# Four small moves in a hybrid encoder block: activation sums, their splits, branch inputs, and an inverse root

## The chip, the cores and the metric

The kernel runs on one core of one Trainium2 chip, as a single launch. The metric is the device time of one execution in microseconds (us). The four names that come up all the time are the engines of the core: PE (TensorE, matmul), DVE (VectorE), ACT (ScalarE) and SP (SyncE, whose queue issues nearly all DMAs of this kernel).

## The reference, cut to what matters

One encoder block on a sequence of 1024 tokens of width 1024, in float32. A normalised input is projected by one wide matrix, the pieces feed a gated linear attention (GLA, branch A) and a windowed softmax attention (SWA, branch B), two sigmoid gates merge the branches, and a SwiGLU follows.

```python
h = rms_norm(x, norm_mix_g)
(g_q, g_k, g_v, g_r, g_lr_f, g_lr_b, s_q, s_k, s_v, gate_a, gate_b) = split(h @ w_in)
y_gla = gla(g_q, g_k, g_v, log gates from g_lr_f and g_lr_b)   # chunks of 64, both directions
y_gla = (rms_norm(y_gla, out_g) * silu(g_r)) @ w_o_gla
y_swa = windowed_softmax_attention(rope(rms_norm(s_q)), rope(rms_norm(s_k)), s_v, sinks) @ w_o_swa
x = x + (sigmoid(gate_a) * y_gla + sigmoid(gate_b) * y_swa) @ w_out
x = x + (silu(h2 @ w_gate) * (h2 @ w_up)) @ w_ffn_out           # h2 = rms_norm(x, norm_ffn_g)
```

## The kernel before

**Matmuls.** Float32 operands are split into a high part `h` (a copy by ACT, rounded to the matmul's type) and a low part `l` (the rest, a subtraction by DVE); a product is three matmuls, high by high, high by low, low by high. A weight tile of 128x512 is loaded (`wr`), split into `wh` and `wl` (`wunit`, L66 to L71) and used. The normalised input lies in 16 pairs of tiles `xh{k}{s}`, `xl{k}{s}` (k is one of 8 blocks of channels, s one of two halves of the tokens).

**Order of the work.** The order of PE's instructions is the order of the program (a manual schedule for PE alone). The orders of DVE, ACT and SP are set by the tile scheduler, which places each instruction by its own model; so an edit can move instructions far from where they are written. Each engine then works through its list in order, and so does SP's queue: a DMA that waits for its data or for a free buffer holds back the DMAs listed after it.

**Dense work as filling.** The wide projections stand in a list `dense` of generators. `fill(n)` takes n matmuls from it; `slot(stages, n)` spreads n such matmuls between the parts of an attention slot. The list ends with `first_halves`, the first half of the gate projections.

**GLA.** 24 dense matmuls run first (`fill(24)`), then the slots. In the first 8 slots `x_sums(t)` loads blocks of x, normalises them (`x_norm`) and forms five sets of sums and differences of blocks (T1, T2, 22, T3, T4) that a Strassen-like scheme needs later; each result goes to memory.

**SWA.** 22 slots; in the last four (t of 18 and more) the stages of the attention drain out, with 15 dense matmuls in each.

**Second halves of the gates.** The five sets, four tiles of 128x512 each, are loaded from memory and split (`xpart`): ACT makes `xh`, DVE `xl`. Before, the sets T1, T2 and 22 are loaded right behind the attention, with `fill(4)` after each tile; then the rest of the dense work; then `second_first(0)`, which loads and combines three weight tiles (`r11`, `r21`, `r22`) and multiplies with T1; then the sets T3 and T4; then eight rounds of `second_rest(f)`. Each round multiplies with T2, 22, T3 and T4 in turn, by weights that DVE combines from the raw ones (`comb`, L808) and `wsplit` splits (ACT L794, DVE L795). `second_rest(f)` calls `second_first(f + 1)` near its end.

**Branch inputs.** After each round, `prep_a(0, f)` loads one tile of GLA's output and one of its gate projection r into two of the four `stage` buffers, takes a sigmoid on ACT (L895), multiplies twice on DVE (L896, L897) and splits the product into `oah`, `oal`. `branch_a`, which comes right after the eight rounds, multiplies by all eight such tiles.

**The inverse root** `rsqrt` (L95 to L102) takes a logarithm and an exponential on ACT and then one Newton step on DVE. It runs twice on 128x512 at the start, and on small tiles in every GLA and SWA unit.

Of the kernel before, what the change touches and what calls it, by code (L numbers as in the profile page):

```python
# [32 lines left out]
def body(tc, i, out):  # L33
    nc = tc.nc
    with ExitStack() as root:
# [8 lines left out]
        def nm(s):  # L44
            uid[0] += 1
            return f"{s}_{uid[0]}"
# [4 lines left out]
        def chtile(shape, dt=F32):  # L51
            return psc.tile(list(shape), dt, tag="ch", name=nm("ch"))
# [41 lines left out]
        def rsqrt(dst, v, scale, epsv, eps_t, pool, shape, tag):  # L94
            l = pool.tile(list(shape), F32, tag=tag + "l", name=nm("rl"))  # L95
            nc.scalar.activation(l, v, AF.Ln, bias=eps_t[:, 0:1], scale=scale)
            nc.scalar.activation(l, l, AF.Exp, scale=-0.5)
            t = pool.tile(list(shape), F32, tag=tag + "t", name=nm("rt"))
            nc.vector.tensor_scalar(t, v, scale, epsv, op0=ALU.mult, op1=ALU.add)
            nc.vector.tensor_tensor(t, t, l, op=ALU.mult)  # L100
            nc.vector.scalar_tensor_tensor(t, t, -0.5, l, op0=ALU.mult, op1=ALU.mult)
            nc.vector.scalar_tensor_tensor(dst, t, 1.5, l, op0=ALU.add, op1=ALU.mult)  # L102


        xstack = ExitStack()
        stg = root.enter_context(tc.tile_pool(name="stg", bufs=4))
        pad = root.enter_context(tc.tile_pool(name="pad", bufs=1, side="right"))
        pad.tile([P, PAD // 4], F32, tag="pad", name="pad")
        xp = xstack.enter_context(tc.tile_pool(name="xp", bufs=1, side="right"))
        xh = [[xp.tile([P, HT], FR, tag=f"xh{k}{s}", name=f"xh{k}{s}") for s in range(2)] for k in range(KT)]  # L110
        xl = [[xp.tile([P, HT], FR, tag=f"xl{k}{s}", name=f"xl{k}{s}") for s in range(2)] for k in range(KT)]

        scr = {}
# [6 lines left out]
        glas = ExitStack()  # L120
# [133 lines left out]
        dense = []  # L254

        def fill(n):

            while n > 0 and dense:
                try:
                    next(dense[0])  # L260
                    n -= 1
                except StopIteration:
                    dense.pop(0)

        def share(plan, t):
            return next(n for end, n in plan if t < end)
# [48 lines left out]
        xr = {}  # L315
# [237 lines left out]
                  proj_t("v1", 1), proj_f("q3", 6), proj_f("k3", 7), proj_t("skv", 2), proj_t("sq0", 3),  # L553
                  proj_t("sq1", 4)] + [proj_f(f"r{m}", 8 + m) for m in range(8)] + [first_halves()]

        xn = glas.enter_context(tc.tile_pool(name="xn", bufs=4))
        part = {}

        def x_norm(k, s):
            t = xn.tile([P, HT], F32, tag="xn", name=nm("xn"))  # L560
            nc.sync.dma_start(out=t, in_=i["xT"][k, s])
            nc.vector.scalar_tensor_tensor(t, t, g1[:, k:k + 1], rstd[:, s * HT:(s + 1) * HT],
                                           op0=ALU.mult, op1=ALU.mult)
            return t
# [5 lines left out]
        def x_sums(j):  # L570
            k, late = divmod(j, 2)
            if not late:
                a, b = part[k] = x_norm(k, 0), x_norm(k, 1)
                x_diff("xT1", k, b, b, a)
                return
            a, b = part.pop(k)
            c = x_norm(k + 4, 1)
            put(("x22", k), c)
            x_diff("xT2", k, b, c, b)
            x_diff("xT3", k, a, b, a)  # L580
            c = x_norm(k + 4, 0)
            x_diff("xT4", k, c, c, b)
# [10 lines left out]
                    at[t, j + (j == 4 and c % 2)] = (f, hd, c)  # L593
                last = max(last, t)
        with tc.manual_schedule(engines={mybir.EngineType.PE}):
            fill(24)
            for t in range(last + 1):
                if t < 8:
                    x_sums(t)
                slot([(lambda v=at[t, j]: v[0](*v[1:])) if (t, j) in at else None for j in (0, 5, 4, 3, 2, 1)], share(GF, t))  # L600
        glas.close()


# [150 lines left out]
        def a_out(g, n):  # L754
# [7 lines left out]
            for h in range(4):  # L762
                nc.sync.dma_start(out=scr["b", 4 * g + h, n // 4][:, (n % 4) * P:(n % 4 + 1) * P],
                                  in_=ob[:, h])

        todo = [[] for _ in range(2 * KT + 6)]
        for n in range(2 * KT):
            g, t = divmod(n, KT)
# [9 lines left out]
        with tc.manual_schedule(engines={mybir.EngineType.PE}):  # L778
            for t, v in enumerate(todo):
                v.sort(key=lambda e: order.index(e[0]))  # L780
                slot([lambda e=e: e[0](*e[1:]) for e in v], share(SF, t))
        swas.close()

        wq = root.enter_context(tc.tile_pool(name="wq", bufs=1))
# [4 lines left out]
        tp = tps.enter_context(tc.tile_pool(name="tp", bufs=1))  # L789
# [21 lines left out]
        def product(o, w, x, nk, start, stop):  # L811
            h, l = w
            for kk in range(nk):
# [1 line left out]
                nc.tensor.matmul(o, h[:, c], x[kk][0], start=start and kk == 0, stop=False, skip_group_check=True)  # L815
                nc.tensor.matmul(o, h[:, c], x[kk][1], start=False, stop=False, skip_group_check=True)  # L816
                nc.tensor.matmul(o, l[:, c], x[kk][0], start=False, stop=kk == nk - 1, skip_group_check=True)  # L817

        XT = {q: [] for q in ("T1", "T2", "22", "T3", "T4")}
        raws = []  # L820

        def xsplit(pool, th, tl, src):
            h = pool.tile([P, HT], FR, tag=th, name=nm(th))
            l = pool.tile([P, HT], FR, tag=tl, name=nm(tl))
            nc.scalar.activation(h, src, AF.Copy)
            nc.vector.tensor_tensor(l, src, h.bitcast(F32), op=ALU.subtract)
            return h, l

        homes = {"T1": (xp, "xh{}1", "xl{}1", 0), "22": (xp, "xh{}1", "xl{}1", 4), "T2": (tp, "t2h{}", "t2l{}", 0),
                 "T3": (xp, "xh{}0", "xl{}0", 0), "T4": (xp, "xh{}0", "xl{}0", 4)}  # L830

        def xpart(q, k):
            r = tp.tile([P, HT], F32, tag="xr", name=nm("xr"), bufs=8)
            nc.sync.dma_start(out=r, in_=scr[f"x{q}", k])
            pool, th, tl, d = homes[q]
            XT[q].append(xsplit(pool, th.format(k + d), tl.format(k + d), r))

        def ntile():
            return tp.tile([P, HT], F32, tag="nt", name=nm("nt"), bufs=6)
# [8 lines left out]
        def second_first(f):  # L848
# [5 lines left out]
            g.Z = chtile((P, HT))  # L854
            product(g.Z, wsplit(g.s1, 512), XT["T1"], 4, True, False)

        def second_rest(f):
            nme, m, a, b = PAIRS[f]
            g = pend.pop(f)
            p1 = ntile()  # L860
            nc.sync.dma_start(out=p1, in_=scr[f"{nme}{m}", "p1"])
            r12 = rawload(i["w_f"][a, 1], False)
            p5 = ntile()
            nc.vector.tensor_tensor(p5, g.Z, p1, op=ALU.add)
            X = mmtile()
# [12 lines left out]
            product(X, wsplit(g.r22, 512), XT["T4"], 4, False, True)  # L878
            result((f"{nme}{m + 4}", 0), X, p1)
# [9 lines left out]
        def prep_a(s, k):  # L889
            o = stage()  # L890
            nc.sync.dma_start(out=o, in_=scr["o", k, s])
            r = stage()
            nc.sync.dma_start(out=r, in_=scr[f"r{k}", s])
            sg = btile("sg", bufs=1)
            nc.scalar.activation(sg, r, AF.Sigmoid)  # L895
            nc.vector.tensor_tensor(r, r, sg, op=ALU.mult)  # L896
            nc.vector.scalar_tensor_tensor(o, o, og[:, k % 2:k % 2 + 1], r, op0=ALU.mult, op1=ALU.mult)  # L897
            oa[s].append(split_in(bo, o, "oa", k))

        with tc.manual_schedule(engines={mybir.EngineType.PE}):  # L900
            for q in ("T1", "T2", "22"):
                for k in range(4):
                    xpart(q, k)
                    fill(4)
            fill(1 << 30)
            second_first(0)
            for q in ("T3", "T4"):
                for k in range(4):
                    xpart(q, k)
            for f in range(len(PAIRS)):  # L910
                second_rest(f)
                prep_a(0, f)
        tps.close()
        xstack.close()

# [443 lines left out]
```

## Time and profile before

| What | Number |
|---|---|
| median of 3 runs | 1684.49 us (1682.74 to 1684.93) |
| profiled execution, its own time | 1679.58 us |
| its span in the trace | 1677.3 us, so 2.28 us lie around it |
| PE busy, share of the span | 1655.2 us, 99% |
| matmuls | 7788 |
| DVE, ACT busy | 1237.9 us (74%), 857.1 us (51%) |
| mean granted PE clock | 0.996 |

A busy PE says little by itself here, since a matmul's end is modelled and a matmul at half the clock counts as busy too. What is to be read is the number of matmuls in a stretch: where PE is never held up, 20 us hold some 90 of them.

### The profile page before, as it was taken

The numbers are of one execution on the slowest core, as the hardware profiler recorded it, in microseconds if no ns is written. First come the engines' busy times: TensorE is split into PE (matmuls) and PEld (weight loads), VectorE is DVE, ScalarE is ACT, GpSimd is POOL, SyncE is SP. The second block draws the span as 40 slices with busy tenths as digits, with TensorE's granted clock in tenths as the row PEclk, the third lists the DMA queues.
The fourth block names the chain that finished last, engine by engine and source line by source line (L and its number), as shares of the span: only waits on it lengthen the run. The fifth ranks groups of instructions, "written<-read, shape, count | busy, mean of one in ns | idle before, by whom it ended". The sixth has DMA issues, their size and how long they took to land.

```text
span 1677.3 us, 23798 instructions
## 1 busy us (share of the span) xinstructions
PE 1655.2 (99%) x7788; PEld 1372.9 (82%) x7788; DVE 1237.9 (74%) x2570; ACT 857.1 (51%) x1809; POOL 0.2 (0%) x4
## 2 busy tenths in 40 slices
PE   9999999999999998999999999999999999999999
PEld 6788888887888876887888888788888888888887
DVE  8786777853997767876673568887778877789755
ACT  7454677865687674334553556533333333344443
POOL 0000000000000000000000000000000000000000
PEclk9999999999999999999999999999999999999999
DMA  8875656668533238656764545344224543595433
GB/s 286 297 259 186 200 185 227 226 196 284 185 108 107 82 113 285 227 193 214 217 213 143 190 134 180 113 136 134 91 92 144 164 157 131 177 323 192 143 102 119
DMA packets 183547, 300.13 MB, mean 179 GB/s; under 512 B 20894, under 2 KB 46238, under 8 KB 183424
## 3 DMA queue, kind: packets, MB, share of 16 engines
q1 hardware_dynamic: 183424, 298.62, 54.4%
q8 instruction: 61, 1.00, 0.3%
q14 instruction: 62, 0.51, 0.1%
HBM read 203.12 MB, written 95.42 MB: 178 GB/s over the span
## 4 chain that ended last, share of the span: by engine, by line
PE 91%; DVE 3%; DMA 3%; ACT 2%; issue 1%; SPq 0%; ACTq 0%; DVEq 0%
PE mm L75 35%; PE ch L75 8%; PE mm L815 7%; PE mm L816 7%; PE mm L817 7%; PE mm L1177 7%; PE ch L1177 5%; PE ch L815 3%; PE ch L817 3%; PE ch L816 3%; PE mm L244 2%; PE ch L747 1%; DMA xr<-xT 1%; PE ch L546 0%; PE ch L697 0%
## 5 line engine op out<-in xcount | busy, mean ns | idle before, releaser
L69 ACT ACTIVATE wh<-wr 128x512 fp32r<-128x512 f32 x198 | 123.8, 628 | 115.1 <-PE mm L75 84.5
L71 DVE TENSOR_TENSOR wl<-wr,wh 128x512 fp32r<-128x512 f32 x198 | 135.7, 686 | 32.0 <-ACT wh L69 29.1
L794 ACT ACTIVATE wh<-ws 128x512 fp32r<-128x512 f32 x120 | 75.5, 631 | 148.7 <-PE mm L816 84.6
L75 PE MATMUL mm<-wl,xh 128*128 128x512 f32 x320 | 127.0, 397 | 1.2 <-DMA wl<-wl 1.2
L75 PE MATMUL mm<-wh,xh 128*128 128x512 f32 x320 | 127.7, 399 | 0.4 <-DVE st L136 0.4
L75 PE MATMUL mm<-wh,xl 128*128 128x512 f32 x320 | 127.9, 400 | 0.0
L75 PE MATMUL mm<-xh,wh 128*128 128x512 f32 x256 | 102.5, 401 | 0.3 <-ACT wh L69 0.3
L75 PE MATMUL mm<-xl,wh 128*128 128x512 f32 x256 | 102.0, 398 | 0.3 <-DVE xl L323 0.3
L794 ACT ACTIVATE wh<-wr 128x512 fp32r<-128x512 f32 x60 | 37.9, 632 | 105.4 <-issue 49.6
L795 DVE TENSOR_TENSOR wl<-ws,wh 128x512 fp32r<-128x512 f32 x120 | 82.1, 685 | 12.8 <-ACT wh L794 12.8
L75 PE MATMUL mm<-xh,wl 128*128 128x512 f32 x256 | 88.6, 399 | 0.0
L794 ACT ACTIVATE wh<-a 128x512 fp32r<-128x512 f32 x66 | 41.7, 632 | 90.6 <-PE mm L1177 42.4
L795 DVE TENSOR_TENSOR wl<-a,wh 128x512 fp32r<-128x512 f32 x66 | 45.5, 690 | 39.2 <-ACT wh L794 38.1
L75 PEld LDWEIGHTS mm<-wl,xh 128*128 128x128 f32 x320 | 60.5, 189 | 12.6 <-DMA wl<-wl 1.6
L75 PEld LDWEIGHTS mm<-wh,xh 128*128 128x128 f32 x320 | 60.7, 190 | 10.5 <-DVE st L136 0.8
L1177 PE MATMUL mm<-hh,wh 128*128 128x512 f32 x176 | 68.6, 390 | 0.5 <-DVE c L1115 0.5
L75 PEld LDWEIGHTS mm<-wh,xl 128*128 128x128 f32 x320 | 60.7, 190 | 10.2
L1177 PE MATMUL mm<-hl,wh 128*128 128x512 f32 x176 | 68.5, 389 | 0.0
L1177 PE MATMUL mm<-hh,wl 128*128 128x512 f32 x176 | 68.5, 389 | 0.0
L1150 DVE TENSOR_TENSOR hl<-hr,hh 128x512 fp32r<-128x512 f32 x77 | 52.7, 686 | 6.8 <-ACT hh L1149 6.7
L75 PEld LDWEIGHTS mm<-xl,wh 128*128 128x128 f32 x256 | 48.2, 188 | 7.6 <-DVE xl L323 0.6
L75 PEld LDWEIGHTS mm<-xh,wh 128*128 128x128 f32 x256 | 48.2, 188 | 7.4 <-ACT wh L69 0.5
(546 smaller groups left out, 4875.0 us busy)
## 6 DMA issues: line engine op xcount, KB each, us to landing
wr<-in_w_fi_dram SPq DMA_DIRECT2D x102, 256.0 KB, 2.8
wr<-in_w_f_dram SPq DMA_DIRECT2D x80, 256.0 KB, 3.4
wh<-wh SPq DMA_DIRECT2D x80, 256.0 KB, 2.9
wl<-wl SPq DMA_DIRECT2D x80, 256.0 KB, 3.0
B<-c SPq DMA_DIRECT2D x44, 256.0 KB, 2.1
T<-st SPq DMA_DIRECT2D x44, 256.0 KB, 2.6
a<-in_w_fo_dram SPq DMA_DIRECT2D x44, 256.0 KB, 5.3
hr<-T SPq DMA_DIRECT2D x44, 256.0 KB, 2.7
```

The costliest lines, as they stand in the source:

```text
L69: nc.scalar.activation(h, raw, AF.Copy)
L71: nc.vector.tensor_tensor(l, raw, h.bitcast(F32), op=ALU.subtract)
L75: nc.tensor.matmul(o, a, b, start=start, stop=stop)
L244: nc.tensor.matmul(Y[q], w[:, c], x, start=f0, stop=f1, skip_group_check=True)
L747: nc.tensor.transpose(pt[:, h], a.p[:, h, (kb - a.b0) * P:(kb - a.b0 + 1) * P], ident)
L794: nc.scalar.activation(h, src, AF.Copy)
L795: nc.vector.tensor_tensor(l, src, h.bitcast(F32), op=ALU.subtract)
L815: nc.tensor.matmul(o, h[:, c], x[kk][0], start=start and kk == 0, stop=False, skip_group_check=True)
L816: nc.tensor.matmul(o, h[:, c], x[kk][1], start=False, stop=False, skip_group_check=True)
L817: nc.tensor.matmul(o, l[:, c], x[kk][0], start=False, stop=kk == nk - 1, skip_group_check=True)
L1150: nc.vector.tensor_tensor(l, r, h.bitcast(F32), op=ALU.subtract)
L1177: nc.tensor.matmul(ys[m], a[:, c], b, start=f0, stop=f1, skip_group_check=True)
```

## The change

1. `rsqrt` makes its Newton step with three DVE instructions in place of four.
2. The pool `xn` (four buffers of 128x512) lives through the whole kernel rather than through GLA alone, and the eight `xr` buffers for the five sets are gone: the sets are now loaded into the four `xn` buffers.
3. GLA starts with `fill(36)` in place of `fill(24)`. `x_sums` is called one slot later, behind the slot rather than ahead of it.
4. T1 and 22 (two of the five sets) are loaded and split in the four drain slots of the softmax attention. Behind the attention only T2 is loaded, with `fill(8)` after each tile.
5. `prep_a(0, f)` is called ahead of `second_rest(f)` rather than behind it, and `prep_a(0, 7)` together with `prep_a(0, 6)`, so the last round runs behind the last branch input.

```diff
-            nc.vector.tensor_scalar(t, v, scale, epsv, op0=ALU.mult, op1=ALU.add)
-            nc.vector.tensor_tensor(t, t, l, op=ALU.mult)
-            nc.vector.scalar_tensor_tensor(t, t, -0.5, l, op0=ALU.mult, op1=ALU.mult)
+            nc.vector.scalar_tensor_tensor(t, l, -0.5 * scale, l, op0=ALU.mult, op1=ALU.mult)
+            nc.vector.scalar_tensor_tensor(t, v, epsv / scale, t, op0=ALU.add, op1=ALU.mult)
             nc.vector.scalar_tensor_tensor(dst, t, 1.5, l, op0=ALU.add, op1=ALU.mult)
...
+        xn = root.enter_context(tc.tile_pool(name="xn", bufs=4))
...
-        xn = glas.enter_context(tc.tile_pool(name="xn", bufs=4))
...
-            fill(24)
+            fill(36)
             for t in range(last + 1):
-                if t < 8:
-                    x_sums(t)
                 slot([...], share(GF, t))
+                if 1 <= t <= 8:
+                    x_sums(t - 1)
...
         def xpart(q, k):
-            r = tp.tile([P, HT], F32, tag="xr", name=nm("xr"), bufs=8)
+            r = xn.tile([P, HT], F32, tag="xn", name=nm("xn"))
             nc.sync.dma_start(out=r, in_=scr[f"x{q}", k])
...
                 slot([lambda e=e: e[0](*e[1:]) for e in v], share(SF, t))
+                if t >= 2 * KT + 2:
+                    assert len(dense) == 1
+                    for q in ("T1", "22"):
+                        xpart(q, t - 2 * KT - 2)
...
-            for q in ("T1", "T2", "22"):
-                for k in range(4):
-                    xpart(q, k)
-                    fill(4)
+            homes["T2"] = tp, "t2h{}", "t2l{}", 0
+            for k in range(4):
+                xpart("T2", k)
+                fill(8)
             fill(1 << 30)
             second_first(0)
             for q in ("T3", "T4"):
                 for k in range(4):
                     xpart(q, k)
             for f in range(len(PAIRS)):
+                if f < 7:
+                    prep_a(0, f)
+                if f == 6:
+                    prep_a(0, 7)
                 second_rest(f)
-                prep_a(0, f)
```

Where the scheduler puts things now is seen at three places.

The first is SP's queue between the attention and the first round. The rows are DMAs, out<-in. Rows of the loads that fetch the sets read `xr<-` before and `xn<-` after (`x_..` is the set 22, `xT_..` the other sets); `wr`, `wr_2...` are weight tiles; `gb_...` are stores of dense results. Before, with the last weight load of `second_first(0)` (`wr_8871`) and the first of `second_rest(0)` (`wr_2162`, r12):

```order
L250 DMA gb_p_8835<-st_8833 128x512
L803 DMA wr_8871<-in_w_f_dram 128x512
L834 DMA xr_8894<-xT_0_721 128x512
L834 DMA xr_8900<-xT_1_933 128x512
L250 DMA gb_0_8851<-st_8849 128x512
L834 DMA xr_8906<-xT_2_1219 128x512
L834 DMA xr_8912<-xT_3_1504 128x512
L250 DMA gb_0_8867<-st_8865 128x512
L834 DMA xr_8918<-xT_0_727 128x512
```

After, with the same weight loads as `wr_8827` and `wr_2167`:

```order
L249 DMA gb_p_8614<-st_8612 128x512
L822 DMA wr_8827<-in_w_f_dram 128x512
L249 DMA gb_p_8648<-st_8646 128x512
L861 DMA nt_8910<-ga_p_8056 128x512
L777 DMA xn_8850<-xT_0_920 128x512
L777 DMA xn_8856<-xT_1_1202 128x512
L249 DMA gb_0_8670<-st_8668 128x512
L777 DMA xn_8862<-xT_2_1493 128x512
L777 DMA xn_8868<-xT_3_1757 128x512
L822 DMA wr_2167_8912<-in_w_f_dram 128x512
```

Behind `gb_p_8634`, the store that corresponds to `gb_p_8614`, the queue before had twelve loads of T1, T2 and 22 and five more stores ahead of `wr_8871`; now the weight load is the very next DMA. The load of r12, which stood behind all eight loads of T3 and T4, stands behind the four of T3. The loads of T1 and 22 are up in the attention and in GLA, and their splits on ACT and DVE lie between earlier units of the attention, before the four drain slots.

The second is ACT between the last rounds and branch A. `sg` is the sigmoid, `oah` the high part of a branch input, `wh<-ws` and `wh<-wr_2...` belong to the rounds, the other `wh<-wr` to branch A. Before:

```order
L794 ACTIVATE wh_9909<-wr_2365_9785 128x512
L69 ACTIVATE wh_9981<-wr_9979 128x512
L69 ACTIVATE wh_9999<-wr_9997 128x512
L895 ACTIVATE sg_9830<-st_9828 128x512
L69 ACTIVATE wh_10022<-wr_10020 128x512
L825 ACTIVATE oah_2376_9834<-st_9826 128x512
L69 ACTIVATE wh_10040<-wr_10038 128x512
L69 ACTIVATE wh_10063<-wr_10061 128x512
L69 ACTIVATE wh_10081<-wr_10079 128x512
L895 ACTIVATE sg_9933<-st_9931 128x512
L825 ACTIVATE oah_2400_9937<-st_9929 128x512
```

After:

```order
L895 ACTIVATE sg_9670<-st_9668 128x512
L813 ACTIVATE wh_9835<-ws_9833 128x512
L768 ACTIVATE oah_2350_9674<-st_9666 128x512
L895 ACTIVATE sg_9682<-st_9680 128x512
L813 ACTIVATE wh_9857<-ws_9855 128x512
L768 ACTIVATE oah_2355_9686<-st_9678 128x512
L813 ACTIVATE wh_9877<-wr_2375_9765 128x512
L69 ACTIVATE wh_9937<-wr_9935 128x512
L69 ACTIVATE wh_9955<-wr_9953 128x512
```

The last two branch inputs came behind weight splits of branch A; now they come ahead of the last round's final three weight splits.

The third is SP between GLA and the softmax attention, where constants of the attention (`cosb` to `sink`), the first keys (`kvr`) and the re-read weights of the projection `sq1` (`wl_..<-wl_2`) stand behind stores of GLA's output. Before, from the first constant on:

```order
L62 DMA cosb<-in_c_cos_dram 128x512
L62 DMA sinb<-in_c_sin_dram 128x512
L62 DMA band<-in_c_band_dram 128x384
L62 DMA qg<-in_qg_dram 128x128
L62 DMA kg<-in_kg_dram 128x128
L62 DMA sink<-in_sink_dram 128x8
L663 DMA kvr_5663<-skv_3683 128x512
L220 DMA sq_0_5704<-st_5705 128x512
L220 DMA sq_1_5714<-st_5715 128x512
L220 DMA sq_2_5724<-st_5725 128x512
L220 DMA sq_3_5734<-st_5735 128x512
L168 DMA wl_5744<-wl_2_5377 128x512
```

After:

```order
L219 DMA sq_0_5595<-st_5596 128x512
L219 DMA sq_1_5693<-st_5694 128x512
L219 DMA sq_2_5703<-st_5704 128x512
L62 DMA cosb<-in_c_cos_dram 128x512
L62 DMA sinb<-in_c_sin_dram 128x512
L62 DMA band<-in_c_band_dram 128x384
L62 DMA qg<-in_qg_dram 128x128
L62 DMA kg<-in_kg_dram 128x128
L62 DMA sink<-in_sink_dram 128x8
L661 DMA kvr_5667<-skv_3606 128x512
L219 DMA sq_3_5713<-st_5714 128x512
L167 DMA wl_5723<-wl_2_5314 128x512
```

Three stores of `sq1` now stand ahead of the constants, and `wl_2` still behind all of them. On PE the dense work is 12 matmuls further on when GLA ends. At the start of GLA, the matmul of the gates (`ch<-lrS,upS`) stands behind 36 dense matmuls rather than 24.

More of the change, by code (lines that the diff above doesn't have):

```diff
@@ L764, in a_out, with xsplit, xpart @@
                                   in_=ob[:, h])
+        XT = {q: [] for q in ("T1", "T2", "22", "T3", "T4")}
+        def xsplit(pool, th, tl, src):
+            h = pool.tile([P, HT], FR, tag=th, name=nm(th))
+            l = pool.tile([P, HT], FR, tag=tl, name=nm(tl))
+            nc.scalar.activation(h, src, AF.Copy)
+            nc.vector.tensor_tensor(l, src, h.bitcast(F32), op=ALU.subtract)
+            return h, l
+        homes = {"T1": (xp, "xh{}1", "xl{}1", 0), "22": (xp, "xh{}1", "xl{}1", 4),
+                 "T3": (xp, "xh{}0", "xl{}0", 0), "T4": (xp, "xh{}0", "xl{}0", 4)}
+        def xpart(q, k):
+            r = xn.tile([P, HT], F32, tag="xn", name=nm("xn"))
+            nc.sync.dma_start(out=r, in_=scr[f"x{q}", k])
+            pool, th, tl, d = homes[q]
+            XT[q].append(xsplit(pool, th.format(k + d), tl.format(k + d), r))
         todo = [[] for _ in range(2 * KT + 6)]
@@ L817, in product @@
                 nc.tensor.matmul(o, l[:, c], x[kk][0], start=False, stop=kk == nk - 1, skip_group_check=True)
[L819 to L832, printed above, removed]
-            r = tp.tile([P, HT], F32, tag="xr", name=nm("xr"), bufs=8)
-            nc.sync.dma_start(out=r, in_=scr[f"x{q}", k])
-            pool, th, tl, d = homes[q]
-            XT[q].append(xsplit(pool, th.format(k + d), tl.format(k + d), r))
         def ntile():
```

## The prediction

> **What bounds the kernel now.** First the page's busy row, then the waits of PE, then PE's matmuls in stretches of 20 us.
>
> ```profile
> PE 1655.2 (99%) x7788; PEld 1372.9 (82%) x7788; DVE 1237.9 (74%) x2570; ACT 857.1 (51%) x1809; POOL 0.2 (0%) x4
> PE ch L815 <- ACT wh L794: 4.6, 2, 2.6
> PE mm L75 <- ACT oah L825: 3.2, 1, 3.2
> PE ch L75 <- DVE lrS L313: 1.9, 1, 1.9
> PE mm L75 <- DMA wl<-wl: 1.2, 1, 1.2
> PE ch L75 <- ACT ph L750: 1.2, 1, 1.2
> 40.00:60.00 20.00, 17.76 (x73) 14.01 (x73) 16.67 (x34) 9.00 (x16) 0.00 (x0) 0.91 0.76 271
> 640.00:660.00 20.00, 17.55 (x77) 13.90 (x76) 15.27 (x25) 10.44 (x18) 0.00 (x0) 1.00 0.92 307
> 660.00:680.00 20.00, 17.42 (x60) 13.41 (x61) 18.18 (x30) 11.31 (x19) 0.00 (x0) 0.83 0.94 312
> 700.00:720.00 20.00, 20.00 (x90) 16.56 (x89) 17.14 (x28) 6.96 (x11) 0.00 (x0) 1.00 0.51 170
> 780.00:800.00 20.00, 16.66 (x66) 13.43 (x67) 13.70 (x21) 10.71 (x18) 0.00 (x0) 0.91 0.85 269
> ```
>
> PE bounds the kernel, and the change removes no matmul, so all that can be won is time in which PE stands still or runs slowly. In a wait row the numbers are the sum, how often, and the longest, in us. The five rows are the longest waits of PE. In a stretch the number behind `x` after PE's busy time is its matmuls, and the third number from the end is the granted clock. Undisturbed, 20 us hold 90 matmuls, 0.222 us each. From 640 to 680 there are 77 + 60, 43 too few, worth 43 x 0.222 = 9.6 us; from 780 to 800 there are 24 too few, 5.3 us; from 40 to 60 there are 17 too few, 3.8 us. That is 18.7 us, while the waits in those places add up to 4.6 + 3.2 + 1.9 = 9.7. Most of the rest is the clock behind the waits, seen in shorter stretches:
>
> ```profile
> 49.65:53.06 3.41, 3.41 (x10) 2.64 (x9) 3.38 (x6) 0.73 (x2) 0.00 (x0) 0.50 0.87 308
> 660.64:664.05 3.41, 3.41 (x10) 2.63 (x9) 2.61 (x5) 1.52 (x4) 0.00 (x0) 0.50 1.00 275
> 670.88:674.29 3.41, 3.41 (x9) 2.67 (x9) 3.41 (x7) 3.38 (x5) 0.00 (x0) 0.50 0.90 272
> 783.52:786.93 3.41, 3.19 (x8) 2.48 (x8) 2.99 (x6) 2.71 (x5) 0.00 (x0) 0.50 0.74 208
> 412.00:415.41 3.41, 2.21 (x10) 1.50 (x10) 2.84 (x12) 0.50 (x2) 0.00 (x0) 1.00 0.96 318
> 700.00:703.41 3.41, 3.41 (x16) 2.82 (x15) 3.37 (x6) 1.71 (x3) 0.00 (x0) 1.00 0.32 119
> ```
>
> Behind each of four waits the clock is halved for 3.41 us, and 8 to 10 matmuls go through where 16 would: on the mean 27 / 4 x 0.222 = 1.5 us lost. The wait at 412 to 414 left the clock at 1.00.
>
> **The splits and the first round (640 to 680).** SP's queue and the work behind the two waits of 4.6 us:
>
> ```profile
> 638.47 0.32 SPq L250 DMA_DIRECT2D gb_p<-st  x1
> 638.96 1.30 SPq L834 DMA_DIRECT2D xr<-xT  x3
> 652.43 0.42 SPq L803 DMA_DIRECT2D wr<-in_w_f_dram  x1
> 662.07 1.85 SPq L803 DMA_DIRECT2D wr<-in_w_f_dram  x4
> 657.26 0.69 DVE L808 TENSOR_TENSOR ws<-wr,wr 128x512 f32<-128x512 f32 x1
> 658.04 0.63 ACT L794 ACTIVATE wh<-ws 128x512 fp32r<-128x512 f32 x1 [2.04 <-DVE ws L808]
> 664.54 2.29 DVE L826 TENSOR_TENSOR xl<-xr,xh 128x512 fp32r<-128x512 f32 x3 [0.16 <-ACT xh L825]
> 667.94 0.68 DVE L808 TENSOR_TENSOR ws<-wr,ws 128x512 f32<-128x512 f32 x1
> 668.72 1.23 ACT L794 ACTIVATE wh<-ws 128x512 fp32r<-128x512 f32 x2 [2.62 <-DVE ws L808]
> ```
>
> PE waits for `wh`, ACT for `ws`, DVE for a weight tile that SP issues at 652.43, behind twelve loads of sets that began at 638.96. In the new order it is the DMA right behind the store of 638.47: it can start some 13 us sooner, and the first wait goes. The second wait is for r12, in the group issued at 662.07 behind all loads of T3 and T4, and for the three `xl` of 664.54 that DVE takes ahead of `ws`. In the new order r12 stands behind four loads, and the eight splits of T1 and 22 are off this stretch altogether: 8 x 0.63 us of ACT (the row of 658.04) and 8 x 0.69 us of DVE. I take both waits and both clock losses as gone: 43 matmuls, 9.6 us, less 0.3 for small ones: 9.3 us. What is late next is T3 and T4, which now share four buffers, so a load waits for a split. T4's first product comes three products (3 x 12 matmuls, 8 us) behind the round's first, and a load with its split takes some 4 to 6 us (652.43 to 658.04), so they fit with little to spare. The first `prep_a`, two loads, a sigmoid and three DVE operations, now falls into this stretch too, where DMA is 0.94 busy.
>
> The moved splits need cover inside the attention:
>
> ```profile
> 580.00:600.00 20.00, 20.00 (x104) 16.73 (x103) 14.60 (x44) 11.69 (x30) 0.00 (x0) 1.00 0.28 84
> 591.26 0.56 DVE L715 CUSTOM_DVE_ANT_0 p<-ch,band 128x384 f32<-128x384 f32 x1 [2.04 <-PE ch L75]
> 596.28 0.60 ACT L700 ACTIVATE sqh<-ch 128x512 fp32r<-128x512 f32 x1 [2.35 <-PE ch L697]
> 440.00:460.00 20.00, 20.00 (x109) 17.25 (x108) 19.78 (x84) 14.06 (x43) 0.00 (x0) 1.00 0.32 94
> ```
>
> From 580 to 600 DVE is free for 5.4 us and ACT for 8.3, in idle pieces of about 2 us, and PE never stops; 5.5 us of DVE over three or so such slots costs nothing. Were they to fall where DVE is full (440 to 460, 19.78 of 20), each would delay the attention by 0.69 us. The final waits for `ph` in the drain (1.2 us) stay: the order of ACT around them is as it was.
>
> **The branch inputs (780 to 800).**
>
> ```profile
> 777.28 2.90 DMA st<-r
> 780.26 0.63 ACT L895 ACTIVATE sg<-st 128x512 f32<-128x512 f32 x1 [1.86 <-DMA st<-r]
> 782.44 0.63 ACT L825 ACTIVATE oah<-st 128x512 fp32r<-128x512 f32 x1 [1.55 <-DVE st L897]
> ```
>
> The last `prep_a` is one chain: load of r, sigmoid, two products, split; PE waits 3.2 us for it. In the new order the last two such chains start a full round earlier (48 matmuls, 48 x 0.222 = 10.7 us), where 3.2 us sooner would do. Both run side by side with all four `stage` buffers, which holds the stores of the round, not PE. All of it goes: 24 matmuls, 5.3 us, less 0.1.
>
> **The start (40 to 60).**
>
> ```profile
> 31.28 0.69 DVE L99 TENSOR_SCALAR rt<-ch 128x512 f32<-128x512 f32 x1
> 47.14 1.21 DVE L313 TENSOR_TENSOR lrS<-lrf,lrS 32x1024 fp32r<-32x1024 f32 x1
> 48.50 0.47 PE L75 MATMUL ch<-lrS,upS 98*128 98x256 f32 x2 [1.89 <-DVE lrS L313]
> ```
>
> Behind the 24 dense matmuls PE waits 1.89 us for `lrS`, ready at 47.14 + 1.21 = 48.35. Twelve more matmuls fill 12 x 0.222 = 2.7 us, which leaves 0.8 us to spare. DVE also has two operations of 0.69 us less to do ahead of `lrS`, which only adds to that. Wait and clock go: 17 matmuls, 3.8 us, of which I take 3.5, since short matmuls are among the missing. The small `rsqrt` calls save one short DVE instruction each; where DVE is not what PE waits for that is nothing, and I count 0.
>
> **What gets worse: the entry to the attention.**
>
> ```profile
> 404.07 0.33 SPq L62 DMA_DIRECT2D cosb<-in_c_cos_dram  x1
> 407.55 2.39 SPq L220 DMA_DIRECT2D sq<-st  x4
> 409.99 4.30 DMA wl<-wl
> 414.33 0.50 PE L75 MATMUL mm<-wl,xh 128*128 128x512 f32 x1 [1.20 <-DMA wl<-wl]
> ```
>
> PE waits here for a low weight tile, issued at 409.99 behind constants whose first (404.07) follows GLA's last output. With the dense work 12 matmuls ahead, PE wants that tile 2.7 us sooner, at 414.33 - 1.20 - 2.7 = 410.4. The tile's load comes sooner by less: three of the four stores that took 2.39 us move ahead of the constants, so I put its issue at 408 to 409 (404.07, seven DMAs to 407.55, then one store) and its landing, 4.30 us on, at 412.3 to 413.3. PE then waits 1.9 to 2.9 us in place of 1.2. From 1.9 us on the clock fell in this trace (the wait for `lrS`), at 1.2 it did not, so another 1.5 goes with it. The bounds are 0.7 without the clock and 3.2 with it; I take 2.4: a wait of 2.1, since the fourth store's data come sooner as well, and the clock.
>
> **The sum.** 9.3 + 5.2 + 3.5 - 2.4 = 15.6 us less. On the profiled execution that is 1679.58 - 15.6 = 1664.0. The median of the runs stands 4.9 above that execution, so on its basis it is 1684.49 - 15.6 = 1668.9 us. A measurement tells about 0.2%, 3.4 us, from no change.
>
> **The rivals.** (a) *One wait in the splits stays.* For it: T3 and T4 go through four buffers beside the first `prep_a`, with DMA at 0.94. Against it: the margin above. One such wait with its clock is half of 9.6 (4.8), so 1668.9 + 4.8 = 1673.7. (b) *The drain or the start gives nothing.* A split put ahead of the last `ph` would add its 0.6 to 0.7 us to a wait of 1.2, and past 2 us add the clock, 1.5; or the start's wait moves to the next gates. That costs 2.2 to 3.5: 1671 to 1672. (c) *The longer wait at the entry leaves the clock whole.* It then costs 0.9 us (2.1 in place of 1.2), and the time is 1684.49 - 18.0 + 0.9 = 1667.4. For it: the wait of 1.2 did so; against it: the one of 1.9 did not. [...] (d) *The weight load does not move in time*: if SP is held at the store of 638.47 or by a buffer, the 9.3 us stay and the time is 1678. (e) *Slower.* The splits sit in ACT's and DVE's order ahead of the parts that PE waits for, and a set's load that SP cannot issue until a split frees a buffer holds the weight loads behind it. If each of the eight splits stopped PE for a load of 3 us and halved the clock (1.5), that is 8 x 4.5 = 36 us, and the time 1684.5 + 36 - 15.6 = 1705. It decides once each split costs over 2 us. The idle pieces of 2 us in both engines speak against it.
>
> **How the numbers follow.** The forecast has 0.45, (c) 0.13, (a) 0.19, (b) 0.12, (d) 0.05, (e) 0.06. Cases (a) to (c) and the forecast are faster, 0.89; (d), 6.5 us below, is faster as well in most runs, so 0.92 faster; 0.03 within 0.2%, from a mild (e); 0.05 slower. The range reaches from 1663, which is (c) less 4 us (the runs before spread by 2.2, and the profiled execution stands 4.9 below their median), to (d), 1678.
>
> **What would show it.** PE's waits for `wh` at the first round, for `oah` and for `lrS` gone, with 88 or more matmuls in each of the matching stretches; no half clock but one, near the entry to the attention; the weight load issued right behind that store; attention slots with 104 to 109 matmuls per 20 us. A half clock left between T2 and T4 would be (a); new PE waits for `sqh` or `ph` between 500 and 630 would be (e).

## The result, and the profile after

| | before | after |
|---|---|---|
| median of 4 runs | 1684.71 us (1682.74 to 1684.95) | 1669.47 us (1667.89 to 1671.38) |
| profiled execution, span | 1679.58, 1677.3 us | 1667.89, 1666.1 us |

The ratio is 0.9912, with a 95% interval of 0.99 to 0.9924: 12.8 to 16.8 us less, where 15.6 was forecast and 1668.9 us predicted. The two profiled executions lie 11.7 us apart (11.2 by their spans): that of before was shorter than all four of its runs, 5 us under their median, that of after 1.6 under.

First the busy row and PE's longest waits after the change, then the stretches that were shown of before.

```profile
PE 1650.8 (99%) x7788; PEld 1370.0 (82%) x7788; DVE 1230.9 (74%) x2525; ACT 857.0 (51%) x1809; POOL 0.2 (0%) x4
PE mm L75 <- DMA wl<-wl: 2.6, 1, 2.6
PE ch L75 <- DVE sh L474: 1.7, 2, 0.9
PE ch L75 <- ACT ph L748: 1.2, 1, 1.2
40.00:60.00 20.00, 20.00 (x91) 16.62 (x91) 15.64 (x32) 9.99 (x18) 0.00 (x0) 1.00 0.86 290
400.00:420.00 20.00, 17.40 (x71) 13.86 (x70) 5.56 (x17) 4.38 (x10) 0.00 (x0) 0.91 0.91 289
640.00:660.00 20.00, 20.00 (x90) 16.57 (x89) 17.14 (x29) 9.18 (x16) 0.00 (x0) 1.00 0.91 289
660.00:680.00 20.00, 19.49 (x86) 15.53 (x85) 17.65 (x29) 11.25 (x18) 0.00 (x0) 1.00 0.84 277
780.00:800.00 20.00, 20.00 (x90) 16.57 (x89) 14.12 (x23) 10.27 (x19) 0.00 (x0) 1.00 0.78 246
```

The waits for `wh` in the first round, for `oah` and for `lrS` are gone from the list. From 640 to 680 PE now does 176 matmuls rather than 137 (39 x 0.222 = 8.7 us), from 780 to 800 it does 90 rather than 66 (5.3 us), from 40 to 60 it does 91 rather than 73 (4.0 us). The entry to the attention got worse: the wait for the low weight tile went from 1.2 to 2.6 us. Before, its stretch was

```profile
400.00:420.00 20.00, 18.80 (x84) 15.25 (x83) 6.66 (x21) 5.41 (x13) 0.00 (x0) 1.00 0.91 296
```

with 84 matmuls where there are 71 now. The chain of the trace after at that place, start and length in us:

```profile
405.67 0.27 SPq L62
409.53 4.34 DMA wl<-wl
413.92 2.09 PE mm L75 x7
```

The load was issued at 409.53 rather than 409.99, while PE wanted it at 413.92 - 2.6 = 411.3 rather than at 414.33 - 1.20 = 413.1, so 1.8 us sooner. The clock was at half for a while behind it (0.91 in the row from 400 to 420).

Where time was won and lost is also seen from when the same matmul starts in the two traces (us). In the first three rows the change has 12 more matmuls behind it, worth 2.7 us, and the last column counts them.

| matmul | before | after | after is ahead by |
|---|---|---|---|
| last pair of GLA (`ch<-ident,ob`) | 400.04 | 400.95 | 1.8 |
| first one with keys in the attention | 439.27 | 443.21 | -1.2 |
| last one of the attention (`ph`) | 633.41 | 638.12 | -2.0 |
| first one with T2 in the first round | 663.78 | 661.26 | 2.5 |
| first one of branch A | 772.10 | 765.90 | 6.2 |
| last one of branch A with `oah` | 910.78 | 899.13 | 11.6 |

So GLA itself got slower: of the 4.0 us won at the start, 1.8 are left at its end. The entry cost 3.0 and the attention 0.8; 8.2 us were won from there to branch A, at the two waits for `wh`, and 5.4 in branch A.

### The profile page after: what moved, and what is told of

Same layout as the page of the kernel before. It is cut to its first block, busy times and chain, and to the rows that moved or that the text cites. A ratio compares the mean times of both kernels' runs of the same rounds, so it can differ in the third digit from the quotient of the medians.

```text
span 1666.1 us, 23707 instructions
## 1 busy us (share of the span) xinstructions
PE 1650.8 (99%) x7788; PEld 1370.0 (82%) x7788; DVE 1230.9 (74%) x2525; ACT 857.0 (51%) x1809; POOL 0.2 (0%) x4
## 4 chain that ended last, share of the span: by engine, by line
PE 86%; DVE 6%; ACT 3%; DMA 3%; issue 1%; SPq 1%; DVEq 0%; ACTq 0%
PE mm L75 33%; PE ch L75 7%; PE mm L1180 7%; PE mm L834 7%; PE mm L835 7%; PE mm L836 7%; PE ch L1180 5%; PE ch L835 3%; PE ch L834 3%; PE ch L836 3%; PE mm L243 2%; PE ch L745 1%; DMA xn<-in_xT_dram 1%; DVE wl L71 0%; DMA wr<-in_w_f_dram 0%
```

## The experiments

All were timed beside the kernel before on the same chip. A ratio is that of medians to before; the interval is 95%.

**b_fill36: one number of the kernel before.** My account of the first wait for `wh` was that SP issued a weight load late, behind twelve loads of sets. This edit, far from that place, moves that weight load ahead of all twelve.

```diff
-            fill(24)
+            fill(36)
```

> The kernel before with only fill(24) made fill(36). In its SP list the last weight load of second_first(0) now stands ahead of the twelve loads of T1, T2 and 22 although all twelve splits are still behind the attention; r12 still stands behind all loads of T3 and T4. Theory A (the place of a weight load in SP's queue makes each wait): the start wait and its half clock go (-3.5 us), the first of the two waits for wh goes with its clock (-4.6), the second stays, the entry wait grows to about 2.7 with a half clock (+2.9): 1684.7 - 5.2 = 1679.5. Rival B (the splits crowding ACT and DVE make the waits, wherever the loads stand): both waits for wh stay, 1684.7 - 0.6 = 1684.1.

Measured: 1687.48 us, ratio 1.0017 (1.0008 to 1.0027). Neither came: slower than before. PE's longest wait, the stretches around it, SP's issues and DVE's work ahead of the wait:

```profile
PE ch L815 <- ACT wh L794: 7.9, 1, 7.9
640.00:660.00 20.00, 20.00 (x89) 16.33 (x87) 14.04 (x23) 8.63 (x15) 0.00 (x0) 1.00 0.81 266
660.00:680.00 20.00, 11.83 (x45) 9.13 (x45) 15.61 (x26) 10.47 (x17) 0.00 (x0) 0.84 0.92 306
646.25 0.38 SPq L803 DMA_DIRECT2D wr<-in_w_f_dram  x1
647.88 1.30 SPq L834 DMA_DIRECT2D xr<-xT  x3
668.41 2.75 SPq L803 DMA_DIRECT2D wr<-in_w_f_dram  x4
671.07 3.20 DVE L826 TENSOR_TENSOR xl<-xr,xh 128x512 fp32r<-128x512 f32 x5 [1.23 <-ACT xh L825]
674.18 0.68 DVE L864 TENSOR_TENSOR nt<-ch,nt 128x512 f32<-128x512 f32 x1
675.38 0.68 DVE L808 TENSOR_TENSOR ws<-wr,ws 128x512 f32<-128x512 f32 x1
```

The weight load (646.25) is ahead of the first set (647.88), and the first wait is gone. But PE only reached the product of 22 sooner and waited there once, for 7.9 us, in place of 4.6 in two: the first wait of before had hidden part of the second. On DVE the last five `xl` come first, then the sum `nt`, then `ws`. At equal matmuls, this trace wins 4.0 us on the trace before between the last matmul of the attention and the first with T2, and loses 5.7 from there to branch A. The waits for `wh` are not the whole loss, though: at the last matmul of the attention this trace was already 6.2 us behind. The start wait for `lrS` is off the list, as the theory said, but a half clock stayed at the start (0.91 over the stretch from 40 to 60), and PE did 84 matmuls there, not 91 as in the change.

**u_split8: the change without its early splits.** T1, T2 and 22 are loaded behind the attention again, through eight buffers of `tp`.

```diff
-                if t >= 2 * KT + 2:
...
-                        xpart(q, t - 2 * KT - 2)
...
-            r = xn.tile([P, HT], F32, tag="xn", name=nm("xn"))
+            r = tp.tile([P, HT], F32, tag="xr", name=nm("xr"), bufs=8)
...
-                xpart("T2", k)
-                fill(8)
+            for q in ("T1", "T2", "22"):
+                for k in range(4):
+                    xpart(q, k)
+                    fill(4)
```

> The changed kernel with T1, T2 and 22 all loaded and split behind the attention again, through eight buffers; the rest of the change stays. Its SP list has the last weight load of second_first(0) ahead of all loads of sets, r12 behind all eight loads of T3 and T4. Theory A (queue place): only the second wait for wh is back, with its half clock: 1669.5 + 4.7 = 1674.2. Rival B (crowding): both are back, 1669.5 + 9.3 = 1678.8. Rival C (early splitting is worth nothing): 1669.5.

Measured: 1678.3 us, ratio 0.9965 (0.9951 to 0.9979). One wait is back, not two, but of the size of both:

```profile
PE ch L830 <- ACT wh L809: 8.3, 1, 8.3
663.51 3.63 DVE L769 TENSOR_TENSOR xl<-xr,xh 128x512 fp32r<-128x512 f32 x5 [0.58 <-ACT xh L768]
667.82 0.69 DVE L860 TENSOR_TENSOR nt<-ch,nt 128x512 f32<-128x512 f32 x1 [0.68 <-DMA nt<-ga_p]
669.63 0.68 DVE L823 TENSOR_TENSOR ws<-wr,ws 128x512 f32<-128x512 f32 x1
```

Undoing the splits costs 0.0053 of the time before (0.9965 - 0.9912), 8.9 us, near the 9.3 I gave them. Why, is the next question.

**u_split8_w: the weight loads asked for first.** The edit adds one call ahead of the splits of u_split8, and `second_first(0)` takes what that call loaded.

```diff
+            early[0] = first_load(0)
             for q in ("T1", "T2", "22"):
```

> The kernel of u_split8 (all twelve splits behind the attention, eight buffers), with the three weight loads of second_first(0) asked for ahead of the splits. In its lists r12 then also stands ahead of all loads of sets, and the sum s4 ahead of all splits on DVE. In u_split8 PE waited once, 8.3 us and a half clock, for wh made from s4. Theory A2 (the place of r12, and of s4 behind it, makes that wait): it goes, and the next is the wait of T3's product for the DVE sum nt behind the last splits, at most 3 us: 1669 to 1673. Rival B (loads and splits cannot be done in time, DMA being 0.90 busy, whatever stands first): a wait of some 8 us stays with another name, 1677 to 1679.

Measured: 1677.46 us, ratio 0.996 (0.9945 to 0.9976). The wait stays, under another name:

```profile
PE ch L830 <- DVE nt L867: 8.6, 1, 8.6
670.97 1.37 DVE L769 TENSOR_TENSOR xl<-xr,xh 128x512 fp32r<-128x512 f32 x2 [1.39 <-ACT xh L768]
673.03 0.69 DVE L867 TENSOR_TENSOR nt<-ch,nt 128x512 f32<-128x512 f32 x1 [0.69 <-DMA nt<-ga_p]
```

With r12 and s4 early, PE waits for `nt`, which must have read the bank before the product of 22 adds to it, and `nt` stands behind eight splits (and then waits 0.69 us more for its own load). So r12's place in SP's queue was not it. Two causes are left: DVE's order, or too little time for all the loads.

**u_split8_late: the loads and splits of T3 and T4 asked for behind s4.**

```diff
-            for q in ("T3", "T4"):
-                for k in range(4):
-                    xpart(q, k)
...
             s4 = comb(r12, s2, ALU.subtract)
+            if f == 0:
+                for q in ("T3", "T4"):
+                    for k in range(4):
+                        xpart(q, k)
```

> The kernel of u_split8 (twelve splits behind the attention, eight buffers) with the loads and splits of T3 and T4 asked for inside the first round, behind s4, in place of ahead of the round. DVE's list then has s4 and the sum nt (which must have read the bank before the product of 22 adds to it) ahead of the eight splits of T3 and T4; in u_split8 and u_split8_w it has them behind. Nothing is split earlier than there, and as many bytes are loaded. Theory A3 (DVE's list order makes the wait of 8 us: nt and s4 stand behind eight splits that wait for loads): it goes, with at most 3 us of waits at T3 and T4 in its place, 1669.5 to 1673. Rival B (loads and splits are too many for the time, whatever the order): 1677 to 1679, the wait now at T3.

Measured: 1676.6 us, ratio 0.9962 (0.9948 to 0.9976). Here `nt` and `ws` stand ahead of the splits, and the wait of 8 us at that place is gone; but the time is that of the rival. PE's list of waits and two of its starts:

```profile
PE ch L830 <- ACT wh L809: 4.5, 2, 4.2
663.13 0.50 PE L830 MATMUL ch<-xh,wh 128*128 128x512 f32 x1 [0.32 <-ACT wh L809]
675.60 0.53 PE L830 MATMUL ch<-xh,wh 128*128 128x512 f32 x1 [4.19 <-ACT wh L809]
660.00:680.00 20.00, 14.36 (x49) 9.37 (x48) 16.94 (x28) 11.39 (x20) 0.00 (x0) 0.91 0.87 303
```

The product of 22 starts after 0.32 us of waiting at 663.13, and then the splits of T3 and T4, and behind them the weights of the next round (4.19 us at 675.60), are late instead. From 660 to 680 there are 49 matmuls, against 45 in u_split8 and in b_fill36. The order chose where the lateness showed and won little.

**u_split: the splits written behind the attention, but through the change's pool.** It is u_split8 without the middle piece of its diff: four buffers of `xn`, which lives through the whole kernel.

> The changed kernel with T1 and 22 loaded and split behind the attention again, but through the four buffers of the change. r12 stands ahead of the loads of T3, s4 ahead of seven of the eight splits of T3 and T4. Theory A2 (place of r12 and s4): no wait over 2 us, 1669.5 to 1672; four buffers do the work, not the earlier splits. Rival B (the eight early splits are what matters): a wait of some 8 us stays, 1677 to 1679.

Measured: 1670.59 us, ratio 0.9915 (0.99 to 0.9931), the same as the whole change (0.9912). Four buffers of `xn` do what eight of `tp` did not, and no split is written earlier. ACT's splits and SP's issues show how:

```profile
573.83 1.14 ACT L768 ACTIVATE xh<-xn 128x512 fp32r<-128x512 f32 x2
575.39 0.62 ACT L768 ACTIVATE xh<-xn 128x512 fp32r<-128x512 f32 x1
576.10 0.62 ACT L768 ACTIVATE xh<-xn 128x512 fp32r<-128x512 f32 x1
580.12 0.93 SPq L777 DMA_DIRECT2D xn<-xT  x2
583.36 1.14 SPq L777 DMA_DIRECT2D xn<-xT  x2
644.69 0.92 SPq L777 DMA_DIRECT2D xn<-x  x2
660.00:680.00 20.00, 18.16 (x78) 14.20 (x77) 17.22 (x29) 11.11 (x18) 0.00 (x0) 1.00 0.91 308
```

The scheduler itself took the four splits of T1 to 574 to 577 us and the four loads of T2 to 580 to 584, some 60 us ahead of where they are written. It can, because the buffers are free then. It did not take 22 along: its loads (`xn<-x`) are issued from 644.69 on and it is split behind them, whereas the change has all eight splits of T1 and 22 between 573 and 601 us, and T2's loads right behind (595 to 604). From 660 to 680 PE does 78 matmuls here and 86 in the change; the medians do not show that difference.

**u_split4tp: the same four buffers, from the pool that opens behind the attention.**

```diff
-            r = xn.tile([P, HT], F32, tag="xn", name=nm("xn"))
+            r = tp.tile([P, HT], F32, tag="xr", name=nm("xr"), bufs=4)
```

> The kernel of u_split (1670.6 us: all twelve splits written behind the attention, four buffers of the pool xn) with its four buffers taken from the pool tp in place of xn. tp is opened behind the attention, in memory that the attention holds until it ends; xn lives all along. In u_split the trace shows four splits at 574 to 577 us and the loads of T2 at 580 to 584, far ahead of where they are written; here no load can be issued before some 640. Theory C (what matters is that the buffers are free early, so that the scheduler can move loads and splits into the attention, not how many there are): PE waits some 8 us again in the first round, 1675 to 1679. Rival (four buffers make the scheduler interleave loads with the sums, and that is enough): 1670 to 1672.

Measured: 1683.46 us, ratio 0.9991 (0.998 to 1.0003), the whole gain lost.

```profile
PE ch L830 <- ACT wh L809: 11.0, 1, 11.0
644.47 1.30 SPq L777 DMA_DIRECT2D xr<-xT  x3
660.00:680.00 20.00, 8.50 (x30) 6.10 (x30) 13.90 (x23) 10.97 (x17) 0.00 (x0) 0.70 0.83 270
```

The first load of a set is issued at 644.47, and PE waits 11.0 us. Against u_split only the pool differs. It went past the 1679 I gave: from this pool, four buffers are worse than eight (1678.3 us in u_split8).

**b_split: the splits alone, on the kernel before.** The pool and the place of the splits are as in the change; all else is as before.

> The kernel before with only the splits moved: pool xn for the whole kernel, T1 and 22 loaded and split in the drain slots, T2 with fill(8). fill(24), x_sums, prep_a and rsqrt are as before. Theory: both waits for wh and their half clocks go, the rest stays: 1684.7 - 9.3 = 1675.4. Rival (the gain needs the other parts, since the lists are set by a scheduler): 1680 or more.

Measured: 1673.43 us, ratio 0.9936 (0.9921 to 0.9951): 10.8 us of gain from this part alone. Not all of it need be the splits: in its trace the wait for `lrS` stayed but the clock behind it did not fall (1.00 from 40 to 60), and in that stretch there are 81 matmuls rather than 73, 1.8 us; from 640 to 680 there are 90 + 85 rather than 137, 8.4 us. The rows for the waits that stayed, `oah` and `lrS`, and the second of these stretches:

```profile
PE mm L75 <- ACT oah L769: 3.5, 1, 3.5
PE ch L75 <- DVE lrS L313: 1.9, 1, 1.9
660.00:680.00 20.00, 19.27 (x85) 15.67 (x84) 17.12 (x29) 8.32 (x13) 0.00 (x0) 1.00 0.80 258
```

**u_prep: the branch inputs behind the rounds again.** The loop of the diff is put back, the rest stays.

> The changed kernel with prep_a(0, f) behind second_rest(f) again, as before. Theory: the wait for oah of 3.2 us and its half clock are back: 1669.5 + 5.3 = 1674.8. Rival (the first prep_a in the crowded stretch costs part of what the last ones win): 1669.5 + 4 or less, and the small stalls of 0.54 and 0.29 us at the first round are gone.

Measured: 1674.17 us, ratio 0.9945 (0.993 to 0.9961), 5.6 us over the change, as the theory had it (5.3).

```profile
PE mm L75 <- ACT oah L768: 3.2, 1, 3.2
PE ch L834 <- DVE nt L864: 1.4, 1, 1.4
776.50:780.50 4.00, 3.75 (x9) 2.76 (x10) 3.79 (x6) 2.53 (x5) 0.00 (x0) 0.61 0.72 220
```

The wait of 3.2 us is back, with the half clock behind it (0.61 over these 4 us). Over the branch inputs, from the first matmul of branch A to the last with `oah`, this trace takes 138.9 us and the change 133.2, so all 5.6 us lie there. The wait for `nt` in the first round is 1.4 us, not smaller than in the change (0.4), so no cost of the first `prep_a` is seen there.

**u_fill: the start with 24 matmuls.** `fill(36)` is set back to `fill(24)` in the changed kernel.

> The changed kernel with fill(24) again; x_sums stays a slot later and rsqrt stays short. Theory (12 matmuls of cover at the start, and the same 12 matmuls make the wait at the entry to the attention longer): a start wait is back, somewhat shorter since DVE has less ahead of lrS (0.7 to 1.9 us, with its half clock if 1.9), and the entry wait is 1.2 to 1.4 us with the clock whole (-2.9): 1669.5 + 3.5 - 2.9 = 1670.1, between 1667.5 and 1670.5. Rival (the later x_sums and the shorter rsqrt alone removed the start wait): 1669.5 - 2.9 = 1666.6.

Measured: 1672.98 us, ratio 0.9934 (0.992 to 0.9947), 3.7 us over the change where 0.6 was expected. The start wait came back as expected, at 1.3 us; the entry wait did not shrink to 1.2, so the 2.9 us that were to be won there are missing, most of the difference.

```profile
PE ch L75 <- DVE lrS L312: 1.3, 1, 1.3
PE mm L75 <- DMA wl<-wl: 2.0, 1, 2.0
414.90:418.90 4.00, 4.00 (x11) 3.18 (x12) 1.93 (x9) 0.00 (x0) 0.00 (x0) 0.57 0.99 322
```

So the entry wait is not a matter of 12 matmuls alone: with the dense work where it was before, PE still waited 2.0 us, and the clock fell (0.57 over the last row). The start wait of 1.3 us, against 1.9, is what the shorter `rsqrt` and the later sums give by themselves.

**u_small: the old `rsqrt` and the old place of `x_sums`.** Both edits are undone in the changed kernel.

> The changed kernel with the old rsqrt (four DVE instructions) and with x_sums ahead of its slot again; fill(36) stays. Theory (both change nothing PE waits for, once 36 matmuls cover the start): the start has the margin of 0.8 us, so no start wait over 0.6 us; 1669.5, within 1668 and 1672. Rival (the later sums keep DVE free in the first GLA slots): 1673 or more, with waits for DVE between 50 and 130 us.

Measured: 1672.75 us, ratio 0.9937 (0.9923 to 0.9951). The intervals of this ratio and of the change's just touch, so between nothing and 8.6 us lie between them. By the ratios the two edits together are worth 4.2 us (0.9937 - 0.9912), by the spans (1668.0 and 1666.1) 1.9. Neither the theory nor the rival is shown. One part is seen: shortly before GLA, PE waits 0.36 us for `st` (L136), as it does before, in b_fill36 and in b_split, and not in the change and u_fill, which have both edits; `lrS` is used at 48.87 rather than 48.29. The larger part lies where neither edit is written: from the first matmul with T2 to branch A this trace takes 106.9 us, the change 104.6. Why, and which of the two edits it is, stays open.

**fix_pool and fix_early: the entry to the attention.** Six constants stand ahead of the low weight tile that PE waits for. One kernel loads them by POOL's queue, the other by SP early in GLA, into memory of their own, which needs a pool that is closed behind the attention.

```diff
-        cosb = load_const(sc_, "cosb", i["c_cos"], (P, KT, 64))
+        cosb = load_const(sc_, "cosb", i["c_cos"], (P, KT, 64), eng=nc.gpsimd)
```

```diff
+                if t == 20:
+                    load_consts()
```

> The changed kernel with the six constants of the softmax attention (cosb, sinb, band, qg, kg, sink) loaded by POOL's queue in place of SP's. The low weight tile that PE waits for at the entry then stands behind the stores of sq1 and one load alone. Theory (it is late because SP's queue holds six loads that wait for GLA's last output): it is issued some 3 us sooner, the wait of 2.6 us and its half clock go, 1669.5 - 4.2 = 1665.3. Rival (DMA is 0.91 busy there and the load is late from that; or the constants come late by POOL and hold the first keys): 1669.5 or slower.

> The changed kernel with the six constants of the softmax attention loaded by SP early in GLA, into memory of their own. SP's queue at the entry then holds the stores of sq1 and one load of keys ahead of the low weight tile, as in fix_pool, but the constants are there long before. Theory: the entry wait falls to about 0.7 us with the clock whole (-3.6) and the keys come no later than in the changed kernel, so no wait for kTl over 0.6: 1669.5 - 3.6 = 1665.9. Rival (keys are late for another reason, the first key load, and the wait moves there as in fix_pool): 1669.

Measured: 1669.65 us, ratio 0.9913 (0.9896 to 0.993), and 1669.77 us, ratio 0.9924 (0.9907 to 0.9941): both the same as the change. The first two rows are of fix_pool, the others of fix_early.

```profile
400.00:420.00 20.00, 19.45 (x87) 15.76 (x86) 5.70 (x18) 4.85 (x11) 3.32 (x6) 1.00 0.91 299
PE ch L75 <- DVE kTl L673: 1.3, 1, 1.3
400.00:420.00 20.00, 19.92 (x90) 16.12 (x89) 7.79 (x25) 6.53 (x16) 0.00 (x0) 1.00 0.94 313
PE ch L75 <- ACT kTh L678: 2.1, 1, 2.1
```

The entry is healed in both, with 87 and 90 matmuls rather than 71 and the clock whole (1.00). Then PE waits for keys, 1.3 and 2.1 us. At the first matmul with keys the traces are 2.9 and 3.2 us ahead of that of the change, at the last one of the attention 0.7 and 0.9; by branch A they are 0.5 and 1.5 behind, of which a wait for DVE's `st` in the rounds (0.9 and 1.6 us) is a part. The times are those of the rivals, though the low weight tile itself did come sooner. No version that beats the change was found.

## Why the prediction was right or wrong

**The sum.** Forecast 15.6 us, measured 12.8 to 16.8. By the rows, 8.7 + 5.3 + 4.0 were won at the three places where 9.3, 5.2 and 3.5 had been put, and 84 - 71 = 13 matmuls (2.9 us) were lost at the entry, where 2.4 had been put. That is 15.1 net, 3.9 more than the spans differ by. By the table of equal matmuls 2.2 of it were lost in GLA, where PE's listed waits grew from 2.0 to 3.1 us (those for `sh` from 1.1 to 1.7), 0.8 in the attention, and the rest in small pieces. The forecast has no term for a slower GLA, and why it is slower is not shown. So the total is right partly by luck: the gain between the medians, 15.2 us, is 3.5 larger than the one between the two profiled executions, and these are one trace each.

**The branch inputs.** Right in mechanism and size; u_prep shows them alone. The margin was larger than a round: the last `oah` is split at 754.3, 11.6 us ahead of branch A's first matmul (765.90).

**The start.** Right: no wait, 91 matmuls. The 36 matmuls were needed, since with 24 a wait of 1.3 us is left. But they alone do not give 91: with the old `rsqrt` and the old place of the sums PE did 87 (u_small) and 84 (b_fill36, with a half clock). So counting the small edits as 0 was too low at this place.

**The splits.** The size was right, and my account of it was wrong. "PE waits for `wh`, ACT for `ws`, DVE for a weight tile that SP issues at 652.43, behind twelve loads" is what the rows say, and the first wait did follow that load's place; but "the first wait goes" was no gain by itself: in b_fill36 the load moved, and 4.0 us won there became 5.7 lost at the second wait. And r12's place was not the second wait's cause: u_split8_w moved r12 and kept the wait. What was too late was the whole row of twenty loads and splits, which could not begin before the attention had given up its memory (first load at 638.96 before, at 647.88 in b_fill36, at 644.47 in u_split4tp). "The eight splits of T1 and 22 are off this stretch altogether" was near to the step that carried the gain: what carries it is loads and splits ahead of the attention's end, through the pool `xn`, free during the attention. In u_split four splits and eight loads did it. Writing the splits into the drain slots gave nothing that the medians show (0.9912 against 0.9915), because the scheduler moves enough by itself. The traces measure this part without the rest, from the first matmul with T2 to the first of branch A, the same 456 matmuls: 108.3 us before; 114.0, 114.0, 114.9 and 113.5 in b_fill36, u_split8, u_split8_w and u_split8_late; 118.7 in u_split4tp; 107.4, 104.4 and 104.6 in u_split, b_split and the change. One reading of the kernel was wrong, on the safe side: T4's product stands four products behind the round's first, not three, since `second_first(f + 1)` comes ahead of it.

**The cover in the attention.** Right: no new waits for `sqh` or `ph`, and `ph` still at 1.2 us.

**The entry.** The wait came as said (1.9 to 2.9 forecast, 2.6 measured), with the half clock (0.91 from 400 to 420), but with some luck. The tile landed at 413.87, later than the 412.3 to 413.3 I gave, since the constants, now behind three stores, began at 405.60 and not at 404.07; PE came at 411.3, later than 410.4, and the two errors nearly cancel. "From 1.9 us on the clock fell" is no rule, as the last section shows: u_split8 waited 2.4 us here and kept its clock (1.00 from 412.4 to 416.4). And "12 matmuls ahead" is not the only reason, as u_fill shows.

**The rivals.** (a) and (d) did not come. (b) did not come as it was written, but its price of 2.2 us was paid in GLA. (e), that splits hold the attention, did not come: the attention lost 0.8 us in all, and no experiment takes the part of the splits out of that. (c) held in some kernels and not in the change.

## What to carry to other kernels

When loads and splits crowd behind a stage, ask first when their buffers become free: a pool that reuses the memory of the stage before was not filled early by any order tried here (first load at 644.47 in u_split4tp), and one that lives longer let the scheduler move the work by itself (four splits by 577 us in u_split). Two waits close behind one another on the bottleneck engine are not two gains; the first hides part of the second, and taking it away alone can win nothing (4.6 us in two became 7.9 in one in b_fill36). Where a scheduler sets the lists, one number can move a load at a far place, so undo each part alone before giving it the credit.

## What the runs showed of the hardware

In these traces the length of a wait does not tell by itself whether the granted clock falls behind it. u_fill waited 2.0 us at its entry, and over the four microseconds from 414.9 the clock was 0.57, with 11 matmuls. Here are stretches behind three other waits: u_split8_late's entry (2.7 us), b_fill36's branch inputs (2.9 us) and b_split's start (1.9 us).

```profile
413.90:417.90 4.00, 3.98 (x17) 3.29 (x18) 2.47 (x12) 0.50 (x2) 0.00 (x0) 1.00 0.94 341
790.70:794.70 4.00, 3.75 (x15) 2.91 (x16) 3.83 (x6) 2.51 (x5) 0.00 (x0) 1.00 0.76 217
49.00:53.00 4.00, 4.00 (x19) 3.33 (x20) 3.96 (x7) 2.18 (x4) 0.00 (x0) 1.00 0.79 273
```

The clock stayed whole in all three, with 15 to 19 matmuls. The kernel before waited the same 1.9 us for `lrS` as b_split did, and its clock was 0.64 from 48.5 to 52.5, with 13 matmuls. So a wait of the same length stood ahead of a whole clock and of a fallen one. Behind three longer ones the clock did fall: 3.2 us in u_prep (0.61), 3.5 us in b_split's branch inputs (0.60 from 774 to 778) and 4.2 us in u_split8_late's first round (0.57 from 675.6 to 679.6). What decides it was not shown.
